# A decoder layer on one core: three pools opened and closed in nested order, TensorE's order in the output projection taken from the program, four late sums formed in the accumulation bank

## The chip, the core and the metric

The kernel runs on one core of one Trainium2 chip. A core has five engines with a queue of instructions each: TensorE (PE, matrix products; its weight loads are shown apart as PEld), VectorE (DVE), ScalarE (ACT), GpSimd (POOL) and SyncE (SP), whose queue here issues the transfers. The metric is the device time of one execution in microseconds (us), as the median of several timed runs. Beside the timed runs there is one profiled execution, whose trace gives each instruction's start and length. SBUF is the core's working memory; PSUM holds the accumulation banks, of which the kernel uses eight of 128x512 float32 (pools `psa` and `psb`, four each).

## What is computed

One layer over 1024 rows (tokens) of width 1024, in float32. Cut to its core:

```python
h = rms_norm(x, mix_norm)
z = h @ w_in                                  # eight groups of columns
o_gla = silu(gr) * rms_norm(gla_chunked(gq, gk, gv, log_a), gla_norm)   # 4 heads
o_swa = swa_sink_attention(rms_norm(sq), rms_norm(sk), sv, sinks)       # 8 heads
x = x + concat([o_gla, o_swa]) @ w_out        # the output projection
h2 = rms_norm(x, ffn_norm)
a, b = split(causal_dwconv(h2 @ w_up, conv_w, conv_b))
return x + (silu(a) * b) @ w_down
```

## The kernel before

**Tiling.** Rows are worked on in eight tiles t = 0 to 7 of 128 rows. A float32 operand is split into a high part (a cast on ACT) and a low part (value minus high part, on DVE or POOL): that is `split` (lines 102 to 107), and every product is three passes (high by high, high by low, low by high). A product of a 128x512 tile with four 128-deep pieces of weight is therefore 12 matmuls.

**Stages.** First the projections of the two mixers with the mixers woven in (the stage of `unit_r`, the gate's projection, is the last of them), then the output projection, then the second norm, then the gated MLP ("up" and "down").

**The output projection** is one level of Strassen's scheme in Winograd's form: rows t = 0..3 and 4..7 are the two halves of the rows, the halves of the inner dimension are the two mixers' outputs, and the halves of the columns are 512 wide. Instead of eight products of quarter size there are seven, P1 to P7, each for i = 0..3 (row tiles i and i + 4). Their left factors are pieces of `o` and sums of them (`o_left`, line 806), their right factors pieces and sums of `w_out`, loaded by `load_local`, `load_b22`, `load_b21`, `load_b22_late`, summed by `wo_sums` and `wo_t4` and split by `o_weight` into the places of O_PLACE (slots 0 to 9 of the weight memory, or pieces (j, i) of the three tiles `ex`). P6, P5 and P3 accumulate onto P1's bank, so that bank must have been read before P6 is written into it.

**Adds.** The residual rows x are loaded into `acc` (`load_acc`, 512 KB for each t), and after each product DVE adds the bank to one half of an `acc` row tile (line 827). `gate_tr` transposes the gated output of tile t (four transposes) and forms for t > 3 the differences and sums that are left factors; `o_sum` and `o_sum4` form and split the others.

**The second norm.** When P3 of i (or P4) has been added, row tile t = i (or i + 4) is complete. `norm2_stat` squares and sums it on ACT, `rms_scale` gives the factor by one small operation on DVE (line 176) and a power on POOL (line 178); `norm2_rows` multiplies row, factor and norm weight; `norm2_tr` transposes the result (eight transposes on PE); for t > 3 `norm2_sums` forms the sums that the up projection, again seven products, needs as right factors: nine operations on DVE, six on ACT, one on POOL. The normalized row tiles share two buffers (tag `n2h`); those of t > 3 are held until their `norm2_sums` has read them. The first products of the up projection are P1 and P2 of column chunks 0 and 1; chunk 0's P3 needs the last `norm2_sums`, that of t = 7.

**What sets the order.** Each piece of work is put down with a due time by `at(time, f, ...)`; times are in units of about 5.2 us, O is the start of the output projection, TU = O + 14 that of the up projection, and TR that of the gate's projection. The program emits pieces by due time; a planner then orders every engine's instructions by its own estimate of when they can run, so that the order on an engine can differ from that of the program unless two instructions are tied (`pin`, `behind`). On the chip every engine runs its queue in that fixed order.

**Memory.** SBUF is a stack from the left and one from the right, in pools that are opened and closed in order. The left pool `gl` holds the mixers' small tiles; when it is closed (`open_acc`, line 702, due at O - 0.05) its place goes to `ex` and to `acc` of t = 0..5. The right pools `gl_q` and `pvg` hold `qo` and `vg`, the mixers' outputs; when they are closed (`open_late`, line 710) their place goes to the last `acc` pair, the third `ex` and, in a pool `ph`, to the normalized rows. A new tile waits for the last readers of the tiles that lay in its place.

Of the kernel before, what the change touches and what calls it, by code (L numbers as in the profile page):

```python
# [17 lines left out]
P = 128  # L18
# [16 lines left out]
def hymba_layer_kernel(ctx, tc, x, mix_norm, w_in, w_alpha2, b_alpha, gla_norm,  # L35
# [19 lines left out]
    def bank(name):  # L55
# [4 lines left out]
        for which, starts in (("a", ("oP1", "oP7_3", "oP4_3", "n2pt_4", "n2pt_5_0", "n2pt_2_1", "n2pt_3")),  # L60
                              ("b", ("oP", "n2pt"))):
            if name.startswith(starts):
                return ps[which].tile([P, 512], F32, tag="b", name=name)
# [80 lines left out]
    def const_a():  # L144
        disti = gl.tile([P, 512], F32, tag="k2", name="disti", bufs=K2)[:, 0:256].bitcast(I32)
# [20 lines left out]
    rn = gl.tile([P, 2, NT], F32, name="rn")  # L166
# [42 lines left out]
    def norm2_stat(t):  # L209
        pn, acc = fin["pn"], fin["acc"][t]  # L210
        h = fin["h", t] = fin["ph"].tile([P, D], F32, tag="n2h", name=f"n2h_{t}", bufs=2)
# [4 lines left out]
    def norm2_rows(t):  # L216
        h, acc, r = fin["h", t], fin["acc"][t], fin["r", t]
        if t % 4 < 3:
            act.activation(h, acc, AF.Copy, scale=r[:, 0:1])
            for c in halves:  # L220
                pool.tensor_mul(h[:, c], h[:, c], fin["ffn"][:, c])  # L221
            return
# [4 lines left out]
    def norm2_tr(t):  # L227
        h = fin["h", t]
        if t < 4:
# [3 lines left out]
            pool.tensor_sub(tr_dst(t, 0, 1, True), b11, tr_dst(t, 0, 0, True).bitcast(F32))  # L233
# [124 lines left out]
    vv = gh.tile([P, NT, P], F32, tag="vv", name="vv", bufs=1)  # L358
# [7 lines left out]
    wa_raw = gl.tile([P, 512], F32, tag="k2", name="wa_raw", bufs=K2)[:, 0:256]  # L366
    pool.memset(wa_raw, 0.0)
    glan = gl.tile([P, 1], F32, name="glan")
# [17 lines left out]
    def k2_tile(name):  # L386
        return gl.tile([P, 512], F32, tag="k2", name=name, bufs=K2)
# [254 lines left out]
    def gla_o(t):  # L642
# [13 lines left out]
        grs[t] = rms_scale(ss, P, 4, f"g{t}", gl, "gr", 8)  # L656
# [9 lines left out]
    def gate_tr(t, gs):  # L666
# [12 lines left out]
        i = t - 4  # L679
        split(l32, big[:, t, 4:8, 0, :], big[:, t, 4:8, 1, :])  # L680
        dve.scalar_tensor_tensor(g32, pv, glan, l32, op0=ALU.mult, op1=ALU.subtract)
        dve.tensor_add(qo[:, i, :], qo[:, i, :], vg[0][:, t, :])
# [18 lines left out]

    def open_acc():
# [3 lines left out]
        fp = ctx.enter_context(tc.tile_pool(name="fp", reuse_waits="tile", bufs=1))  # L706
        fin["pair"] = [fp.tile([P, 2, D], F32, name=f"acc{i}") for i in range(3)]
        fin["acc"] = [fin["pair"][t // 2][:, t % 2, :] for t in range(6)]

    def open_late():  # L710
        st.close()
        x2 = ctx.enter_context(tc.tile_pool(name="x2", reuse_waits="tile", bufs=1))
        fin["pair"].append(x2.tile([P, 2, D], F32, name="acc3"))
        fin["acc"] += [fin["pair"][3][:, t, :] for t in range(2)]
        fin["ex"].append(x2.tile([P, 4, 4, 2, P], F32R, name="ex2"))
        fin["sn"] = ExitStack()
# [757 lines left out]
```

## Time and profile before

| what | us |
|---|---|
| median of the timed runs | 1005.75 (1005.57 to 1005.81, 3 runs) |
| the profiled execution, its own time | 1004.07 |
| its span in the trace | 1002.4 |
| PE busy in the span | 974.7 |
| PE busy in the 100 us from 300 to 400 | 85.1 |
| PE busy in the 100 us from 500 to 600 | 100.0 |

The page of the profile shows one execution: busy time by engine, the span in 40 slices (each digit a tenth), the transfers, the chain of work that ended last, and the costliest groups of instructions. A line such as "L821" is line 821 of the kernel. In the timeline and the groups a release in brackets, as in "[5.37 <-DVE acc L827]", is the time for which the engine stood idle before the piece and what ended that wait. PE's matmuls are pipelined, so their durations overlap; the distance from start to start is what one costs. "PEclk" is the clock that PE was granted, as a share of full speed.

### The profile page before, as it was taken

Reading aid. Unit: us, or ns where it says so; the run is one execution under the profiler, and the core shown is the slowest. Engines: PE = TensorE matmul, PEld = TensorE weight load, DVE = VectorE, ACT = ScalarE, POOL = GpSimd, SP = SyncE. Lnnn points to the kernel's source line nnn. Section 1 sums busy time; section 2 is a strip of 40 time slices with the busy share of each in tenths; the row PEclk is TensorE's granted clock in tenths of the full one; section 3 lists DMA queues with packets and bytes.
Section 4 is the critical chain, followed back from the end, with each engine's and each line's share of the span. In section 5 each row is a group of like instructions: output and inputs, shape, how many; then the busy total and the mean of one; then the engine's idle time right before and its main releaser. Section 6 shows DMA issues by size and latency. Waiting matters only on the chain.

```text
span 1002.4 us, 13932 instructions
## 1 busy us (share of the span) xinstructions
PE 974.7 (97%) x4915; PEld 844.4 (84%) x4915; DVE 815.6 (81%) x1350; ACT 506.7 (51%) x1035; POOL 673.4 (67%) x557
## 2 busy tenths in 40 slices
PE   8999999999997978999999999999999999999998
PEld 6888888888886866878888888888888888888887
DVE  6877767766468567698998989898989999898986
ACT  5637655445354356554454545545454545455451
POOL 5593132324687556787889788787878797888760
PEclk9999999999998988999999999999999999999999
DMA  6152123032007201211112221212121212222104
GB/s 225 64 151 73 46 55 93 22 86 64 1 1 275 62 0 43 85 35 59 41 60 60 65 63 43 84 43 84 43 69 37 64 42 65 63 64 63 43 22 168
DMA packets 67540, 68.23 MB, mean 68 GB/s; under 512 B 4650, under 2 KB 52237, under 8 KB 67470
## 3 DMA queue, kind: packets, MB, share of 16 engines
q1 hardware_dynamic: 63484, 62.35, 20.2%
q10 hardware_dynamic: 3986, 4.99, 2.1%
q8 instruction: 39, 0.64, 0.3%
q14 instruction: 31, 0.25, 0.1%
HBM read 58.41 MB, written 4.19 MB: 62 GB/s over the span
## 4 chain that ended last, share of the span: by engine, by line
PE 75%; DVE 9%; POOL 7%; issue 3%; DMA 3%; ACT 2%; ACTq 0%; SPq 0%; POOLq 0%; DVEq 0%
PE fb L969 35%; PE dn_P L1150 17%; PE dg L350 4%; PE dr L350 4%; PE dv L350 3%; PE oP L821 2%; PE pv L536 1%; PE dl L1179 1%; PE fb L1179 1%; DVE ex L107 1%; DMA qraw<-in_w_in_dram 1%; POOL n2h L221 1%; PE go L646 1%; PE ga L637 1%; POOL ex L107 1%
## 5 line engine op out<-in xcount | busy, mean ns | idle before, releaser
L1150 PE MATMUL dn_P<-dw,dg 128*128 128x512 f32 x840 | 205.1, 381 | 1.4 <-DVE acc L1154 0.7
L1154 DVE TENSOR_TENSOR acc<-acc,dn_P 128x1024 f32<-128x1024 f32 x140 | 169.3, 1210 | 30.9 <-PE dn_P L1150 30.9
L1150 PEld LDWEIGHTS dn_P<-dw,dg 128*128 128x128 f32 x840 | 157.2, 189 | 27.5 <-DVE acc L1154 3.2
L107 POOL TENSOR_TENSOR dw<-dn,dw 128x512 fp32r<-128x512 f32 x50 | 64.6, 1291 | 35.6 <-ACT dw L104 35.6
L976 DVE SCALAR_TENSOR_TENSOR ua<-fb,cc,ua 128x511 f32<-128x511 f32 (+1 forms) x84 | 61.8, 739 | 1.2 <-ACT ua L981 0.8
L969 PE MATMUL fb<-big,A11w 128*128 128x512 f32 x252 | 58.8, 381 | 1.1 <-ACT e L1025 1.1
L969 PE MATMUL fb<-big,S1w 128*128 128x512 f32 x252 | 58.6, 379 | 0.0
L969 PE MATMUL fb<-big,A12w 128*128 128x512 f32 x252 | 58.2, 379 | 0.1
L969 PE MATMUL fb<-big,S4w 128*128 128x512 f32 x252 | 58.1, 379 | 0.0
L512 POOL TENSOR_TENSOR pr<-pr,sm 128x512 f32<-128x512 f32 x16 | 17.3, 1080 | 60.7 <-DVE sm L511 33.9
L969 PE MATMUL fb<-ex,S2w 128*128 128x512 f32 x252 | 58.0, 379 | 0.0
L969 PE MATMUL fb<-ex,S3w 128*128 128x512 f32 x252 | 57.8, 379 | 0.0
L969 PE MATMUL fb<-ex,A22w 128*128 128x512 f32 x252 | 57.8, 379 | 0.0
L981 ACT ACTIVATE ua<-fb,cc 128x512 f32<-128x512 f32 x42 | 32.7, 778 | 46.2 <-DVE fb L1029 30.1
L969 PEld LDWEIGHTS fb<-big,A11w 128*128 128x128 f32 x252 | 47.7, 190 | 8.2 <-ACT e L1025 1.5
L969 PEld LDWEIGHTS fb<-big,A12w 128*128 128x128 f32 x252 | 47.5, 189 | 7.0 <-ACT b L232 0.3
L969 PEld LDWEIGHTS fb<-ex,S2w 128*128 128x128 f32 x252 | 47.6, 189 | 6.8
L969 PEld LDWEIGHTS fb<-big,S1w 128*128 128x128 f32 x252 | 47.6, 189 | 6.8
L969 PEld LDWEIGHTS fb<-ex,S3w 128*128 128x128 f32 x252 | 47.6, 189 | 6.8
L969 PEld LDWEIGHTS fb<-big,S4w 128*128 128x128 f32 x252 | 47.6, 189 | 6.8
L969 PEld LDWEIGHTS fb<-ex,A22w 128*128 128x128 f32 x252 | 47.6, 189 | 6.8
L107 POOL TENSOR_TENSOR A22w<-up,A22w 128x512 fp32r<-128x512 f32 x22 | 30.0, 1364 | 31.4 <-ACT A22w L104 31.3
(486 smaller groups left out, 2596.8 us busy)
## 6 DMA issues: line engine op xcount, KB each, us to landing
up<-in_w_up_dram SPq DMA_DIRECT2D x44, 512.0 KB, 3.9
dn<-in_w_down_dram SPq DMA_DIRECT2D x22, 512.0 KB, 3.4
acc<-in_x_dram SPq DMA_DIRECT2D x8, 512.0 KB, 6.1
out_dram<-acc SPq DMA_DIRECT2D x15, 256.0 KB, 2.7
xt<-in_x_dram SPq DMA_DIRECT2D x7, 512.0 KB, 3.4
vraw<-in_w_in_dram SPq DMA_DIRECT2D x4, 512.0 KB, 3.7
graw<-in_w_in_dram SPq DMA_DIRECT2D x4, 512.0 KB, 3.8
qt<-qt ACTq DMA_DIRECT2D x16, 128.0 KB, 2.2
```

The source lines that it names most:

```text
L107: (eng or pool).tensor_sub(lo, src, hi.bitcast(F32))
L221: pool.tensor_mul(h[:, c], h[:, c], fin["ffn"][:, c])
L350: pe.matmul(pb[:, :n], lhsT=big[:, t, k, ra, :], rhs=two_streams(ws[k][:, rb, :n]), start=(k == 0 and i == 0), stop=(k == KD - 1 and i == 2))
L512: pool.tensor_tensor(pr, pr, den[:, hs].rearrange("p (j o) -> p j o", o=1).broadcast_to((P, 4, P)), ALU.mult)
L536: pe.matmul(pbs[i][HALF[g]], lhsT=vv[rows, t - 1 + b, HALF[g]], rhs=rhs[rows, :, HALF[i]], start=start, stop=stop)
L821: pe.matmul(pb, lhsT=left[:, k, ra, :], rhs=two_streams(ow[name, k][:, rb, :]), start=(onto is None and k == 0 and n == 0), stop=(k == 3 a ...
L969: pe.matmul(pb, lhsT=w[:, ra, k, :], rhs=b_operand(bn, k, rb).rearrange("p t (h c) -> p t c h", h=2), start=(onto is None and i == 0), sto ...
L976: dve.scalar_tensor_tensor(dst, src, w, dst, op0=ALU.mult, op1=ALU.add)
L981: act.activation(u[:, a:z], y[:, a:z], AF.Identity, bias=b, scale=w2)
L1150: pe.matmul(pb[:, i], lhsT=g[:, ra, c:c + P], rhs=two_streams(w[:, rb, :]), start=(onto is None and n == 0), stop=(n == 2), skip_group_che ...
L1154: dve.tensor_add(acc, acc, pb.rearrange("p i (c h) -> p i h c", h=2))
L1179: pe.matmul(pb[:, c0:c1], lhsT=g[:, ra, (t % 4) * P:(t % 4 + 1) * P], rhs=two_streams(w[:, rb, c0:c1]), start=(ch == NCH - 2 and i == 0), ...
```

## The change

The pools: `open_acc` moves from O - 0.05 to TR + 2.0. So that `gl` can be closed then, four kinds of small tiles with late readers (`k2`, `rn`, `glan`, the factors `gr`) move into the right pool `gh`, and `vv` moves from `gh` into `gl`. In its place `xp` holds two `ex` tiles and `acc` of t = 0..3; `acc` of t = 4..7 and the third `ex` come in `x2`, opened at O + 2.2; the normalized rows are in `pn`, opened at O + 4.2. Rows 0 to 3 of x are loaded from TR + 2.05, rows 4 to 7 from O + 2.25; the adds of P7 for i = 0 and 1 are put behind that (`o_adds`). P1's weights are split at TR + 2.2 into pieces of `ex`. The loads of B21 and the late B22 are due at O + 4.3 and O + 4.4.

The late sums: for t > 3 `gate_tr` subtracts in the bank itself, splits from it the left factor of P6, and adds and subtracts the bank to `qo` and `vg`. The splits of that factor in `o_sum` and the four subtractions on POOL in `o_sum4` go.

The norm: `norm2_rows` is now two operations of DVE (row by factor by weight) for every t; before, for t % 4 < 3, it was one on ACT and two on POOL. For t = 3 one low part goes from POOL to DVE.

The order: from O to TU + 0.07 each PE instruction is tied to the one before it in the program, so that PE's order there is that of the due times. The transposes of the second norm get due times of their own, and those of the gate's last tile come between P1 of i = 1 and P1 of i = 2.

The diff, with lines of context left out:

```diff
-        for which, starts in (("a", ("oP1", "oP7_3", "oP4_3", "n2pt_4", "n2pt_5_0", "n2pt_2_1", "n2pt_3")),
+        for which, starts in (("a", ("oP1", "oP4_3", "n2pt_4", "n2pt_5_0", "n2pt_3")),
...
     def const_a():
-        disti = gl.tile([P, 512], F32, tag="k2", name="disti", bufs=K2)[:, 0:256].bitcast(I32)
+        disti = gh.tile([P, 512], F32, tag="k2", name="disti", bufs=K2)[:, 0:256].bitcast(I32)
...
-    rn = gl.tile([P, 2, NT], F32, name="rn")
+    rn = gh.tile([P, 2, NT], F32, name="rn")
...
         pn, acc = fin["pn"], fin["acc"][t]
-        h = fin["h", t] = fin["ph"].tile([P, D], F32, tag="n2h", name=f"n2h_{t}", bufs=2)
+        h = fin["h", t] = pn.tile([P, D], F32, tag="n2h", name=f"n2h_{t}", bufs=2)
...
         h, acc, r = fin["h", t], fin["acc"][t], fin["r", t]
-        if t % 4 < 3:
-            act.activation(h, acc, AF.Copy, scale=r[:, 0:1])
-            for c in halves:
-                pool.tensor_mul(h[:, c], h[:, c], fin["ffn"][:, c])
-            return
...
             act.copy(b11, trs["n2", t, 0])
-            pool.tensor_sub(tr_dst(t, 0, 1, True), b11, tr_dst(t, 0, 0, True).bitcast(F32))
+            if t < 3:
+                pool.tensor_sub(tr_dst(t, 0, 1, True), b11, tr_dst(t, 0, 0, True).bitcast(F32))
+            else:
+                tr_lo(t, 0, "n2", True)
...
     la = gh.tile([P, NT, 256], F32, tag="la", name="la", bufs=1)
-    vv = gh.tile([P, NT, P], F32, tag="vv", name="vv", bufs=1)
+    vv = gl.tile([P, NT, P], F32, name="vv")
...
     wa = gl.tile([P, 256], F32R, name="wa")
-    wa_raw = gl.tile([P, 512], F32, tag="k2", name="wa_raw", bufs=K2)[:, 0:256]
+    wa_raw = gh.tile([P, 512], F32, tag="k2", name="wa_raw", bufs=K2)[:, 0:256]
     pool.memset(wa_raw, 0.0)
-    glan = gl.tile([P, 1], F32, name="glan")
+    glan = gh.tile([P, 1], F32, name="glan")
...
     def k2_tile(name):
-        return gl.tile([P, 512], F32, tag="k2", name=name, bufs=K2)
+        return gh.tile([P, 512], F32, tag="k2", name=name, bufs=K2)
...
         dve.tensor_copy(v, pb)
-        grs[t] = rms_scale(ss, P, 4, f"g{t}", gl, "gr", 8)
+        grs[t] = rms_scale(ss, P, 4, f"g{t}", gh, "gr", 8)
...
         i = t - 4
+        dve.scalar_tensor_tensor(pv, pv, glan, l32, op0=ALU.mult, op1=ALU.subtract)
+        s2 = fin["ex"][1][:, (i + 2) % 4]
+        split(pv, s2[:, :, 0], s2[:, :, 1], dve)
         split(l32, big[:, t, 4:8, 0, :], big[:, t, 4:8, 1, :])
-        dve.scalar_tensor_tensor(g32, pv, glan, l32, op0=ALU.mult, op1=ALU.subtract)
-        dve.tensor_add(qo[:, i, :], qo[:, i, :], vg[0][:, t, :])
+        dve.tensor_add(qo[:, i, :], pb, qo[:, i, :])
+        dve.tensor_sub(vg[0][:, i, :], vg[0][:, i, :], pb)
...
+    def open_pair(pl, i):
+        fin["pair", i] = pl.tile([P, 2, D], F32, name=f"acc{i}")
+        fin["acc"][2 * i:2 * i + 2] = [fin["pair", i][:, t, :] for t in range(2)]
+
...
         fin["ex"] = [xp.tile([P, 4, 4, 2, P], F32R, name=f"ex{j}") for j in range(2)]
-        fp = ctx.enter_context(tc.tile_pool(name="fp", reuse_waits="tile", bufs=1))
-        fin["pair"] = [fp.tile([P, 2, D], F32, name=f"acc{i}") for i in range(3)]
-        fin["acc"] = [fin["pair"][t // 2][:, t % 2, :] for t in range(6)]
+        fin["acc"] = [None] * NT
+        for i in range(2):
+            open_pair(xp, i)
...
         x2 = ctx.enter_context(tc.tile_pool(name="x2", reuse_waits="tile", bufs=1))
-        fin["pair"].append(x2.tile([P, 2, D], F32, name="acc3"))
-        fin["acc"] += [fin["pair"][3][:, t, :] for t in range(2)]
+        for i in range(2, 4):
+            open_pair(x2, i)
         fin["ex"].append(x2.tile([P, 4, 4, 2, P], F32R, name="ex2"))
-        fin["sn"] = ExitStack()
-        fin["ph"] = fin["sn"].enter_context(tc.tile_pool(name="ph", reuse_waits="tile", bufs=1))
...
         w_late["pool"] = swp.enter_context(tc.tile_pool(name="wb", reuse_waits="tile", bufs=1, side="right"))
+        fin["sn"] = ExitStack()
...
     def load_b22(c2):
-        load_gated("T1", 1, c2, raw_tile("wog1") if c2 else gh.tile([P, 1024], F32, tag="vv", name="wog0", bufs=1))
+        load_gated("B22", 1, c2, raw_tile(f"wog{c2}"))
...
     def wo_sums(k2):
-        dve.tensor_sub(wo["T3", k2], wo["T1", k2], wo["T3", k2])
+        b22 = wo["B22", k2]
+        dve.tensor_sub(wo["T3", k2], b22, wo["T3", k2])
...
         dve.tensor_add(t2, wo["T3", k2], wo["B11", k2])
-        dve.tensor_sub(wo["T1", k2], wo["T1", k2], t2)
+        dve.tensor_sub(wo["B11", k2], b22, t2)
...
     def load_b21(c2):
-        load_gated("B21", 0, c2, fin["ph"].tile([P, D], F32, tag="n2h", name=f"wob21_{c2}", bufs=2))
+        load_gated("B21", 0, c2, fin["pn"].tile([P, D], F32, tag="n2h", name=f"wob21_{c2}", bufs=2))
...
-    O_PLACE = {"P1": (4, 5, 6, 7), "P7": (8, 0, 1, 2), "P6": (4, 5, 6, 7), "P5": ((2, 0), (2, 1), (1, 3), 3),
-               "P2": (4, 5, 6, 7), "P3": ((0, 2), (2, 2), (1, 2), (0, 3)), "P4": (3, 9, (2, 3), (1, 3))}
-    O_FROM = {"P1": "B11", "P6": "T2", "P5": "T1", "P7": "T3", "P4": "T2", "P2": "B21", "P3": "B22"}
+    O_PLACE = {"P1": ((0, 0), (0, 1), (0, 2), (0, 3)), "P7": (8, 0, 1, 2), "P6": (3, 4, 5, 6),
+               "P5": (7, (1, 2), (1, 3), (2, 0)), "P2": (3, 4, 5, 6), "P3": ((0, 2), (2, 2), (1, 2), (0, 3)),
+               "P4": (7, 9, (2, 3), (1, 3))}
+    O_FROM = {"P1": "B11", "P6": "T2", "P5": "B11", "P7": "T3", "P4": "T2", "P2": "B21", "P3": "B22"}
...
-    def o_sum(j, i):
-        src = (qo[:, i, :], vg[0][:, i + 4, :])[j].rearrange("p (k c) -> p k c", k=4)
-        dst = fin["ex"][j][:, (i + 2) % 4]
-        split(src, dst[:, :, 0], dst[:, :, 1], dve)
+    def o_sum1(i):
+        dst = fin["ex"][0][:, (i + 2) % 4]
+        split(qo[:, i, :].rearrange("p (k c) -> p k c", k=4), dst[:, :, 0], dst[:, :, 1], dve)
...
     def o_sum4(i):
-        pool.tensor_sub(vg[0][:, i, :], vg[0][:, i, :], vg[0][:, i + 4, :])
...
-        def add(t, half):
-            part = fin["acc"][t][:, half * 512:half * 512 + 512].rearrange("p (h c) -> p h c", h=2)
-            dve.tensor_add(part, part, halves_of(pb))
-
+        if (name, i) not in (("P7", 0), ("P7", 1)):
+            o_adds(name, i, pb)
+
+    def o_adds(name, i, pb=None):
+        if pb is None:
+            pb = psb["o", name, i]
...
                          "P7": ((4, 1), (4, 0)), "P4": ((4, 0),)}[name]:
-            add(i + dt, half)
+            part = fin["acc"][i + dt][:, half * 512:half * 512 + 512].rearrange("p (h c) -> p h c", h=2)
+            dve.tensor_add(part, part, halves_of(pb))
...
         t = 4 * th + 2 * j
-        acc = fin["pair"][t // 2][:, :, nh * 512:(nh + 1) * 512].rearrange("p i (h c) -> p i h c", h=2)
+        acc = fin["pair", t // 2][:, :, nh * 512:(nh + 1) * 512].rearrange("p i (h c) -> p i h c", h=2)
...
         at(TR + t, unit_r, t)
-        at(O + (0.005 * t - 0.045 if t < 6 else 2.4), load_acc, t)
+        if t < 4:
+            at(TR + 2.05 + 0.01 * t, load_acc, t)
+        else:
+            at(O + 2.25 + 0.005 * t, load_acc, t)
...
         at(s + 2.7, gla_o, t)
-        at(TR + t + 1.3, lambda tt=t: gate_tr(tt, psb.pop(("r", tt))))
-    at(O - 0.05, open_acc)
+        at(TR + t + 1.3 if t < 7 else O + 0.75, lambda tt=t: gate_tr(tt, psb.pop(("r", tt))))
+    at(TR + 2.0, open_acc)
     for k2 in range(2):
-        at(TR + 1.6 + 0.2 * k2, load_local, k2)
-        at(TR + 1.7 + 0.2 * k2, load_b22, k2)
-        at(TR + 2.3 + 0.2 * k2, wo_sums, k2)
-        at(O + 2.35, load_b21, k2)
-        at(O + 3.35, load_b22_late, k2)
-        at(O + 5.3, wo_t4, k2)
-    at(O + 2.3, open_late)
-    at(O + 3.3, open_norm2)
-    at(O + 3.4, load_ffn)
+        at(TR + 1.6 + 0.05 * k2, load_local, k2)
+        at(TR + 1.7 + 0.9 * k2, load_b22, k2)
+        at(TR + 2.5 + 0.7 * k2, wo_sums, k2)
+        at(O + 4.3 + 0.02 * k2, load_b21, k2)
+        at(O + 4.4, load_b22_late, k2)
+        at(O + 5.4, wo_t4, k2)
+    at(O + 2.2, open_late)
+    at(O + 4.2, open_norm2)
+    at(O + 4.5, load_ffn)
...
         eng = dve if k % 2 else pool
-        at(TO - 0.9 + 0.1 * k, o_weight, "P1", k, dve)
-        at(TO - 0.45 + 0.1 * k, o_weight, "P7", k, eng)
-        at(O + 2.02 + 0.05 * k, o_weight, "P6", k, eng)
-        at(O + (4.02 if k == 2 else 3.02 + 0.05 * k), o_weight, "P5", k, pool)
+        at(TR + 2.2 + 0.05 * k, o_weight, "P1", k, dve)
+        at(TO - 0.6 + 0.1 * k, o_weight, "P7", k, eng)
+        at(TO + 0.1 * k, o_weight, "P6", k, eng)
+        at(O + (2.3, 3.52, 4.02, 3.0)[k], o_weight, "P5", k, pool)
         at(O + 5.02 + 0.05 * k, o_weight, "P2", k, pool)
-        at(O + 6.02 + 0.05 * k, o_weight, "P3", k, eng)
+        at(O + (7.01 if k == 2 else 6.02 + 0.05 * k), o_weight, "P3", k, dve if k == 2 else eng)
...
         at(O + 0.5 * i, o_product, "P1", i)
-        at(O + 0.51 + 0.02 * i, o_sum, 1, i)
-        at(O + 1.51 + 0.02 * i, o_sum, 0, i)
-        at(O + 2.2 + 0.02 * i, o_sum4, i)
+        at(O + 2.02 + 0.02 * i, o_sum1, i)
+        at(O + 0.51 + 0.5 * i, o_sum4, i)
...
             at(O + 2 + 0.5 * i, o_product, "P7", i)
+            at(O + 2.6 + 0.05 * i, o_adds, "P7", i)
...
             at(u + 0.005, norm2_rows, t)
-            if t < 7:
-                at(u + 1.4, norm2_tr, t)
-            if 4 <= t < 7:
-                at(u + 1.51, norm2_sums, t)
+    for t, n in ((0, 19), (4, 20), (1, 22), (5, 24), (2, 26), (6, 27), (3, 28)):
+        at(O + 0.5 * n - 0.002, norm2_tr, t)
+        if t > 3:
+            at(O + 0.5 * n + 0.01, norm2_sums, t)
...
     at_us(-12, behind, first_sums)
-    at_us(0.28, norm2_tr, 7)
+    at_us(0.15, norm2_tr, 7)
...
         tu += MM
-    for _, _, f, a in sorted(ev, key=lambda e: e[:2]):
+    last_pe = None
+    for time, _, f, a in sorted(ev, key=lambda e: e[:2]):
+        n = len(nc.cur_bb.bb.instructions)
         f(*a)
+        if O <= time < TU + 0.07:
+            for ins in nc.cur_bb.bb.instructions[n:]:
+                if ins.engine == mybir.EngineType.PE:
+                    if last_pe:
+                        tc.add_manual_dep(ins, last_pe, mybir.DependencyInfo(
+                            mybir.DependencyClass.NoSync, mybir.DependencyReason.DATA), reason="order of the program")
+                    last_pe = ins.name
```

## The prediction

> **What bounds the kernel now.** I read the page first: engines, then slices, then the stretches around the slices that stand out.
>
> ```profile
> span 1002.4 us, 13932 instructions
> ...
> PE   8999999999997978999999999999999999999998
> ...
> PEclk9999999999998988999999999999999999999999
> ```
> ```profile
> 300.00:350.00 50.00, 44.63 (x203) 38.52 (x202) 36.77 (x46) 21.04 (x38) 33.11 (x24) 0.93 0.48 168
> 350.00:400.00 50.00, 40.44 (x186) 33.92 (x185) 34.43 (x56) 31.45 (x56) 32.42 (x28) 0.86 0.07 22
> ...
> 500.00:600.00 100.00, 100.00 (x463) 87.07 (x463) 91.22 (x119) 51.28 (x87) 82.48 (x62) 1.00 0.22 64
> ```
>
> PE is the bound: it is full in the MLP (100.00 of 100), and the diff leaves the matmuls alone. The stretch from 300 to 400, output projection and second norm, is the exception: 14.9 us idle, and the granted clock falls to 0.86. The waits of PE there name three causes:
>
> ```profile
> PE oP L821 <- DVE acc L827: 5.4, 1, 5.4
> PE n2pt L242 <- POOL n2h L221: 4.9, 1, 4.9
> PE n2pt L276 <- DVE n2h L224: 4.5, 2, 3.4
> ```
>
> So PE waits 5.4 us for an add of residual rows, then 9.4 us for normalized rows. PE's timeline tells what the stretch would take without them:
>
> ```profile
> 289.24 8.23 PE L821 MATMUL oP<-oP1w,big 128*128 128x512 f32 x37
> ...
> 310.83 12.49 PE L821 MATMUL oP<-oP6w,ex 128*128 128x512 f32 x48 [5.37 <-DVE acc L827]
> ...
> 333.53 2.75 PE L821 MATMUL oP<-oP2w,big 128*128 128x512 f32 x12
> 336.12 2.75 PE L821 MATMUL oP<-ex,big 128*128 128x512 f32 x12
> ...
> 358.59 1.04 PE L276 MATMUL n2pt<-ident,n2h 128*128 128x128 f32 x8
> 359.38 2.84 PE L821 MATMUL oP<-oP2w,big 128*128 128x512 f32 x12
> ...
> 396.24 1.04 PE L242 MATMUL fb<-ident,n2h 128*128 128x128 f32 x8
> ```
>
> From start to start a product costs 2.59 (333.53 to 336.12), eight transposes 0.79 (358.59 to 359.38). P6 and P5, eight products after the first wait, should take 20.72 and take 22.70 (310.83 to 333.53): 1.98 lost to the slower clock. From the first P1 to the end of the last tile's transposes 107.8 us pass (289.24 to 397.03). In them are 28 products (72.5), four transposes of the gate (0.4), 21 matmuls of the up projection (4.5) and 64 transposes (6.3): 83.7. So **24 us are lost, 14.8 idle and 9.3 to clock**. That is the most the change can win.
>
> **The change part by part.** *Earlier residual rows.* The rows of the first wait:
>
> ```profile
> SPq L811 <- DVE vg L681: 55.2, 1, 55.2
> ```
> ```profile
> 301.24 2.96 SPq L811 DMA_DIRECT2D acc<-in_x_dram  x6
> 314.36 0.89 SPq L760 DMA_DIRECT2D wob<-in_w_out_dram  x2
> ```
> ```profile
> acc<-in_x_dram SPq DMA_DIRECT2D x8, 512.0 KB, 6.1
> ```
> ```profile
> 255.79 1.06 PE L649 MATMUL go<-s_mid,qbd 128*128 128x128 f32 x8
> ```
>
> SP sat 55.2 us on the first load because `glan`, in the pool to be closed, was read last by line 681. Landing takes 6.1 us, and DVE adds P1 only then. With the late readers in another pool, the last readers of `gl` are the mixer of t = 7, whose matmuls end at 256.8: x lands some 20 us before P1 starts. What now queues behind these four loads on SP is `wog1`, which P7's weights need some 20 us later: covered. P1's four splits move to that time too, beside the gate's products. P6 follows P7 directly, at 289.24 + 6 products + 0.36 = 305.1 instead of 310.83. Rows 4 to 7 wait for `vg`, whose last reader is the last `o_sum4`: line 681 ends at 301.2 now, as the issue shows, and a cast and a split follow, so I take 303; they land by 309, and P5, their first taker, starts at 315.5. The six us between cover a DVE queue that stands at P7's deferred adds. If the cover went, P5 would stall by the excess.
>
> *Late sums.* POOL loses four subtractions, DVE gets four from the bank and loses none of its splits: 4 x 0.60 on DVE beside PE's products, nothing on the path. The gate's last transposes move behind the second P1 (294.4) and need `gs` of POOL:
>
> ```profile
> 293.84 1.73 POOL L663 TENSOR_TENSOR gs<-gs,vg 128x512 f32<-128x512 f32 x1
> ```
>
> It ends at 295.6 now, with subtractions of the removed kind ahead of it. Between no wait and 1.2 us I take none.
>
> *Later weights.* B21's load moves from `qo`'s place into `gh`'s, which is free when P5's weights have been split. Its queue on SP has x ahead of it and B22, the norm weight and the MLP's first columns behind. The second P6 ends at 310.3, and a POOL split follows, so I put the issue at 312 instead of 314.36: 2.4 earlier, where PE comes 5.7 earlier still. The chain behind it is POOL's:
>
> ```profile
> 319.54 4.79 POOL L778 TENSOR_TENSOR wot<-wob,wot 128x1024 f32<-128x1024 f32 x2
> ...
> 331.83 2.52 POOL L107 TENSOR_TENSOR ex<-wob,ex 128x512 fp32r<-128x512 f32 x2
> ...
> 335.59 1.63 POOL L107 TENSOR_TENSOR oP4w<-wot,oP4w 128x512 fp32r<-128x512 f32 x1 [1.25 <-ACT oP4w L104]
> ```
>
> P4's last POOL weight ended at 337.2. Shifted by 2.4 and with one of P3's POOL splits (1.3, half of the 2.52) given to DVE it ends at 333.5; PE wants it at 331.0 as the first piece, at 332.3 as the third. Bounds 0 and 2.5; I take **1.6** of delay for all that follows.
>
> *Rows of the norm, and DVE.* ACT loses six copies and POOL twelve multiplications; DVE gets twelve operations. With stall and slow clock gone PE needs per i three and a half products and two sets of transposes, 10.6 us. What DVE needs:
>
> ```profile
> 355.61 0.70 DVE L259 TENSOR_TENSOR n2pt<-n2pt,b 128x512 f32<-128x512 f32 x1 [1.58 <-ACT n2h L257]
> 356.22 0.68 DVE L107 TENSOR_TENSOR big<-n2pt,big 128x512 fp32r<-128x512 f32 x1
> ...
> 383.93 3.42 DVE L224 SCALAR_TENSOR_TENSOR n2h<-acc,n23r,ffn 128x512 f32<-128x512 f32 x2 [0.84 <-POOL n23r L178]
> ...
> 390.93 1.41 DVE L224 SCALAR_TENSOR_TENSOR n2h<-acc,n27r,ffn 128x512 f32<-128x512 f32 x2
> 392.25 0.69 DVE L259 TENSOR_TENSOR n2pt<-n2pt,b 128x512 f32<-128x512 f32 x1
> ...
> 398.81 0.69 DVE L259 TENSOR_TENSOR fb<-fb,b 128x512 f32<-128x512 f32 x1
> ```
> ```profile
> 386.76 2.95 POOL L221 TENSOR_TENSOR n2h<-n2h,ffn 128x512 f32<-128x512 f32 x2
> 390.08 0.55 POOL L178 TENSOR_TENSOR n27r<-n27v,mhalf 128x1 f32<-128x1 f32 x1 [0.37 <-DVE n27v L176]
> 396.87 1.27 POOL L107 TENSOR_TENSOR ex<-n2h,ex 128x512 fp32r<-128x512 f32 x1 [6.24 <-ACT ex L104]
> ```
>
> An operation from the bank costs 0.60 from start to start; a row operation 0.66 when POOL idles (two in 1.32 at 390.93) and 1.71 when POOL works beside it (383.93). [...]
>
> The mark is the first DVE operation of the last `norm2_sums`, at 398.81 now, since the MLP hangs on it:
>
> ```profile
> 403.37 1.28 POOL L107 TENSOR_TENSOR ex<-n2h,ex 128x512 fp32r<-128x512 f32 x1 [3.97 <-ACT ex L104]
> 404.72 1.28 POOL L903 TENSOR_TENSOR S<-up 128x512 f32<-128x512 f32 x1
> ```
> ```profile
> 411.03 2.75 PE L969 MATMUL fb<-ex,S2w 128*128 128x512 f32 x12
> ```
>
> POOL splits that tile's sum, at once begins chunk 1's sums, and PE's P6 of chunk 1 starts 12.2 us after the mark. Whatever PE gains before, from here it moves with the mark.
>
> When does DVE reach it? PE comes to the transposes of t = 4 after 20 products, 0.36 and 0.79, at 289.24 + 53.0 + 1.6 = 343.8, and their first sum runs 1.2 later, at 345.0. From there to the mark DVE has 27 operations of three `norm2_sums` (16.2), four low parts (2.4), nine adds (5.4), eleven row operations (7.3), five small ones (0.4) and two weight splits (1.2): **32.9**, to 377.9. Thirteen of these read SBUF twice and cost 1.05 more beside POOL: between 0 and 13.6. POOL has about a quarter of that time filled for certain (powers, lows, one split for each tile) and up to half with the MLP's first weights; at 30% it is **4.0**. The mark falls at 381.9, **16.9 earlier**. PE's path alone would bring it at about 374.8, 24 earlier.
>
> Sum: 1004.07 - 16.9 = 987.2 for the profiled execution; the median of the runs stood 1.7 above it, so 1005.75 - 16.9 = **988.9 us**.
>
> **The rivals.** *PE stays the bound.* DVE's row operations find POOL idle and use the gaps before 345; the mark is then PE's, and all 24 us are won: 981.7. For it: DVE stood idle for 15.6 of the 50 us from 350 to 400. Against: per i DVE has 11.3 us of work (nine sums 5.4, four rows 2.6, four adds 2.4, lows and small ones 0.9), 15.5 when the rows meet POOL, against PE's 10.6.
>
> *The first wait is replaced and nothing is won.* The gate's last tile waits for `gs` as long as P6 did (7.4 with the clock), and all thirteen operations meet POOL: 377.9 + 7.4 + 13.6 = 398.9, 1005.8. Against it: `gs` is 1.2 late at most by its row.
>
> *Slower: the two buffers.* Beside the rows above it needs these:
>
> ```profile
> L213 ACT ACTIVATE n2h<-acc 128x1024 f32<-128x1024 f32 x8 | 8.5, 1062 | 8.2 <-DVE acc L827 6.6 <-PE n2pt L276 1.6
> ```
> ```profile
> 368.95 0.70 DVE L259 TENSOR_TENSOR n2pt<-n2pt,b 128x512 f32<-128x512 f32 x1 [2.00 <-ACT n2h L257]
> ```
>
> The row tiles share two buffers, and a tile of t > 3 holds one until its sums are done. If the fixed order leaves tiles 4, 5, 6, 7 following each other in one buffer, each step is sums, POOL's split, square, power, rows and transposes: 5.4 + 1.3 + 1.1 + 0.6 + 3.4 + 1.8 = 13.6 when the rows meet POOL, plus what DVE does in between. The mark is 345.0 plus three steps, so it is later than 398.81 from a step of 17.9 on. At 19.3 it is 402.9: 1009.8. For it: the sums of t = 4, 5, 6 started at 355.61, 368.95 and 392.25, steps of 13.3 and 23.3. Against: the next was 6.6, so tile 7 had the other buffer.
>
> **How the numbers follow.** Forecast with its bounds (mark from 377.9 to 391.5, and up to 0.9 later with P4's upper bound): 984.9 to 999.3, chance 0.65. PE-bound: 0.15. Replaced wait: 0.10, half of it within 2 us of the old time, half a small gain. Slower: 0.10. A difference of 0.2%, 2 us, is what a measurement of this kernel can tell. So faster 0.85, same 0.05, slower 0.10. Forecast and PE-bound case together hold 0.80: the range is 982 to 999.
>
> **What would show it.** Right: the wait for `acc` is gone; PE's order is P1, P1, the gate's transposes, P1, P1, P7; DVE is over 85% busy from 345 to the mark; the remaining waits of PE are transposes that wait for L224 and the first up product after the last sums. Wrong: a long wait for P2's or P4's weights, PE waiting at the gate's transposes, or a square that waits for a row buffer. If POOL's splits of the MLP's weights all fall between 345 and 382, the time is nearer 995.

## The result, and the profile after

| | before | after |
|---|---|---|
| median of the timed runs, us | 1005.64 (1003.72 to 1005.81, 5 runs) | 1000.15 (998.75 to 1001.43, 5 runs) |
| ratio | | 0.9947, interval 0.9932 to 0.9962 |
| the profiled execution, its span | 1004.07, 1002.4 | 1001.43, 999.7 |

The change makes the kernel 5.5 us faster. The forecast was 988.9 us, with a range of 982 to 999: the sign was right, the size is a third of the 16.9 us.

The windows of the changed kernel (columns: stretch, its length, busy time of PE, PEld, DVE, ACT, POOL, granted clock, DMA share, GB/s):

```profile
300.00:350.00 50.00, 48.68 (x230) 41.49 (x229) 33.36 (x46) 19.23 (x35) 25.92 (x19) 1.00 0.34 116
350.00:400.00 50.00, 40.38 (x185) 33.68 (x184) 45.10 (x71) 26.77 (x50) 17.32 (x16) 0.90 0.08 22
500.00:600.00 100.00, 100.00 (x465) 87.22 (x464) 91.36 (x119) 50.16 (x85) 84.86 (x64) 1.00 0.20 58
```

The first half is healed: PE is busy for 48.68 of 50 us, where it was 44.63, at full clock. The second half is as it was: 40.38, where it was 40.44, while DVE rose from 34.43 to 45.10 and POOL fell from 32.42 to 17.32. PE's waits of the changed kernel (total, number, longest) say for what:

```profile
PE n2pt L240 <- DVE n2h L219: 5.7, 4, 2.5
PE fb L274 <- DVE n2h L219: 3.3, 1, 3.3
PE n2pt L274 <- DVE n2h L219: 1.2, 1, 1.2
...
PE ogt L667 <- POOL gs L661: 0.7, 1, 0.7
PE oP L825 <- DVE acc L838: 0.6, 1, 0.6
```

The wait of 5.4 us for an add has gone; 0.7 at the gate and 0.6 at an add have come. The waits of transposes for normalized rows were 4.9 and 4.5, 9.4 in all, and are 5.7, 3.3 and 1.2: 10.2. They are all on DVE now.

PE's timeline of the changed kernel:

```profile
290.76 5.43 PE L825 MATMUL oP<-ex,big 128*128 128x512 f32 x24
296.85 0.66 PE L667 MATMUL ogt<-ident,gs 128*128 128x128 f32 x4 [0.67 <-POOL gs L661]
...
307.71 10.52 PE L825 MATMUL oP<-oP6w,ex 128*128 128x512 f32 x48
...
328.43 2.75 PE L825 MATMUL oP<-oP2w,big 128*128 128x512 f32 x12
...
333.89 1.79 PE L825 MATMUL oP<-oP4w,big 128*128 128x512 f32 x6
...
343.34 1.29 PE L274 MATMUL n2pt<-ident,n2h 128*128 128x128 f32 x8 [1.18 <-DVE n2h L219]
...
347.05 1.28 PE L240 MATMUL n2pt<-ident,n2h 128*128 128x128 f32 x8
...
384.89 1.94 PE L274 MATMUL fb<-ident,n2h 128*128 128x128 f32 x8 [3.33 <-DVE n2h L219]
386.65 4.94 PE L976 MATMUL gb<-big,A11w 128*128 128x512 f32 x12
391.43 2.75 PE L976 MATMUL gb<-big,A12w 128*128 128x512 f32 x12
394.02 1.04 PE L240 MATMUL fb<-ident,n2h 128*128 128x128 f32 x8
...
407.85 2.75 PE L976 MATMUL fb<-ex,S2w 128*128 128x512 f32 x12
```

P6 comes without a wait. The transposes of t = 4 are at 347.05. From those of t = 3 at 384.89 on, PE no longer stands: they, not the last sums, are where the end is set.

One measure serves for all kernels below: **the stretch** from PE's first P1 to its P6 of chunk 1, 290.76 to 407.85 here. It is counted from P1 because P1's own start scatters: it was 290.76 in this profile and 289.23 in a second one of the same kernel. In the stretch lie 28 products and seven up products at 2.59 (90.7), 64 transposes (6.3) and the gate's four (0.4): 97.3 of work at full clock. What goes beyond is lost: in PE's waits, to a lower granted clock, and in small gaps that the list of waits leaves out. That is 24.5 us before (121.8 less 97.3), of which 14.8 are waits; 19.8 after (117.1 less 97.3), of which 11.5 are waits.

DVE's timeline of the changed kernel shows why PE waits:

```profile
332.04 1.10 DVE L107 TENSOR_TENSOR A11w<-up,A11w 128x512 fp32r<-128x512 f32 x1 [1.82 <-ACT A11w L104]
...
334.76 0.68 DVE L107 TENSOR_TENSOR A12w<-up,A12w 128x512 fp32r<-128x512 f32 x1
...
338.29 0.69 DVE L910 TENSOR_TENSOR s<-up 128x512 f32<-128x512 f32 x1 [2.25 <-DMA up<-in_w_up_dram]
...
339.69 0.68 DVE L838 TENSOR_TENSOR acc<-acc,oP 128x512 f32<-128x512 f32 x1
...
342.44 1.42 DVE L219 SCALAR_TENSOR_TENSOR n2h<-acc,n20r,ffn 128x512 f32<-128x512 f32 x2
...
344.59 2.44 DVE L219 SCALAR_TENSOR_TENSOR n2h<-acc,n24r,ffn 128x512 f32<-128x512 f32 x2
...
348.92 0.15 DVE L176 TENSOR_SCALAR n21v<-n2ss 128x1 f32<-128x1 f32 x1 [1.30 <-ACT n2h L213]
...
350.01 1.40 DVE L219 SCALAR_TENSOR_TENSOR n2h<-acc,n21r,ffn 128x512 f32<-128x512 f32 x2
...
352.52 0.69 DVE L257 TENSOR_TENSOR n2pt<-n2pt,b 128x512 f32<-128x512 f32 x1
...
373.15 3.36 DVE L219 SCALAR_TENSOR_TENSOR n2h<-acc,n26r,ffn 128x512 f32<-128x512 f32 x2
...
384.00 1.41 DVE L219 SCALAR_TENSOR_TENSOR n2h<-acc,n23r,ffn 128x512 f32<-128x512 f32 x2
```

The product that completes row tile 0 ends at 333.9 on PE. Its add waits until 339.69, because DVE's queue stands at work for the MLP: at the split of A11 (`up_operand`) for 1.82 us, then at `first_sums` for 2.25 us, until a load of `w_up` has landed. SP issues that load late:

```profile
334.31 0.99 SPq L898 DMA_DIRECT2D up<-in_w_up_dram  x2
```

PE takes nothing of that work before 386.65; the first to read one of the sums is ACT's cast of S4, at 370.67. Behind it the row's square, power, row operations and transposes all come late; PE waits 1.18 at 343.34. The first sums, those of t = 4, begin at 352.52, where the forecast had 345.0. That is 5.5 us behind their transposes: until then DVE is at adds, at a wait of 1.30 for the square of t = 1, and at the rows of t = 1.

### The profile page after: what moved, and what is told of

It reads as the page before. It is cut to its first block, busy times and chain, and to the rows that moved or that the text cites. A ratio compares the mean times of both kernels' runs of the same rounds, so it can differ in the third digit from the quotient of the medians.

```text
span 999.7 us, 13937 instructions
## 1 busy us (share of the span) xinstructions
PE 974.2 (97%) x4915; PEld 842.5 (84%) x4915; DVE 825.3 (83%) x1368; ACT 500.0 (50%) x1029; POOL 647.5 (65%) x539
## 4 chain that ended last, share of the span: by engine, by line
PE 77%; DVE 9%; POOL 5%; issue 3%; DMA 2%; ACT 2%; ACTq 0%; SPq 0%; POOLq 0%; DVEq 0%
PE fb L976 35%; PE dn_P L1157 17%; PE dg L348 4%; PE dr L348 4%; PE dv L348 3%; PE oP L825 3%; PE pv L534 1%; DVE n2h L219 1%; PE dl L1186 1%; PE fb L1186 1%; PE dq L848 1%; DMA up<-in_w_up_dram 1%; PE go L644 1%; PE ga L635 1%; DMA wob<-in_w_out_dram 1%
## 5 line engine op out<-in xcount | busy, mean ns | idle before, releaser
L107 POOL TENSOR_TENSOR dw<-dn,dw 128x512 fp32r<-128x512 f32 x50 | 64.6, 1292 | 35.6 <-ACT dw L104 35.6
L510 POOL TENSOR_TENSOR pr<-pr,sm 128x512 f32<-128x512 f32 x16 | 17.3, 1080 | 61.4 <-DVE sm L509 36.0
```

The lines of the kernel that those rows point to most:

```text
L107: (eng or pool).tensor_sub(lo, src, hi.bitcast(F32))
L510: pool.tensor_tensor(pr, pr, den[:, hs].rearrange("p (j o) -> p j o", o=1).broadcast_to((P, 4, P)), ALU.mult)
```

## The experiments

Three theories stood after the result. **A**: the rows given to DVE fill it, and back on ACT and POOL they would cost less; its rival is that the way of one row (square, factor, rows, transposes) counts, which the change shortens. **B**: the loss is the place of the transposes of t = 7, behind two up products. **C**: the loss is the blocked head of DVE's queue near 335. The ratios are to the kernel before, timed beside each. The stretch comes from each profile; "lost" is the stretch less 97.3, "waits" the sum of PE's waits in it. In the stretch of "PE's order not tied" lie 14 more matmuls of the up projection, 3.0 us, which are taken off too.

| kernel | median us | ratio, interval | stretch | lost | waits |
|---|---|---|---|---|---|
| before | 1005.64 | | 121.8 | 24.5 | 14.8 |
| after | 1000.15 | 0.9947 [0.9932, 0.9962] | 117.1 | 19.8 | 11.5 |
| after, once more | 1000.74 | 0.9935 [0.9913, 0.9956] | 117.6 | 20.3 | 12.1 |
| residual rows late again | 1007.83 | 1.0026 [1.0013, 1.0039] | 123.3 | 26.0 | 15.9 |
| rows on ACT and POOL again | 1002.00 | 0.9961 [0.9944, 0.9978] | 119.2 | 21.9 | 13.7 |
| PE's order not tied | 999.22 | 0.9950 [0.9936, 0.9964] | 117.6 | 17.3 | 11.1 |
| transposes of t = 7 earlier | 998.04 | 0.9936 [0.9911, 0.9961] | 115.5 | 18.2 | 12.5 |
| rows plain | 994.81 | 0.9894 [0.9867, 0.9921] | 112.7 | 15.4 | 10.3 |
| MLP work tied behind the rows | 993.99 | 0.9895 [0.9872, 0.9918] | 111.5 | 14.2 | 8.4 |
| tied, and rows plain | 991.51 | 0.9872 [0.9856, 0.9888] | 109.2 | 11.9 | 6.9 |
| tied, sums on POOL | 997.81 | 0.9929 [0.9914, 0.9944] | 115.0 | 17.7 | 9.4 |
| tied, and t = 7 earlier | 996.29 | 0.9890 [0.9868, 0.9911] | 113.0 | 15.7 | 9.7 |
| before, tied | 1007.28 | 1.0001 [0.9982, 1.0020] | 122.7 | 25.4 | 15.2 |

### The residual rows late again

```diff
-        if (name, i) not in (("P7", 0), ("P7", 1)):
+        if name != "P1" and (name, i) not in (("P7", 0), ("P7", 1)):
...
-            at(TR + 2.05 + 0.01 * t, load_acc, t)
+            at(O + 2.28 + 0.005 * t, load_acc_tied, t)
...
+        at(O + 2.4 + 0.01 * i, o_adds, "P1", i)
```

> The changed kernel with the first part undone: rows 0 to 3 of x are loaded among rows 4 to 7, behind the last readers of vg, and P1's adds come after that. P6 then waits 4 to 7 us for P1's add again. If the chain behind is rigid, all of it arrives: 5 to 8 us slower than the changed kernel, which is what the first part is worth. If DVE's first complete row tile waits for the MLP's weights anyway (theory C), the delay is partly covered: only 1 to 3 us slower.

Measured: 1.0026. PE's timeline of this kernel has the old wait back:

```profile
311.02 4.60 PE L825 MATMUL oP<-oP6w,ex 128*128 128x512 f32 x10 [4.68 <-DVE acc L838]
```

The 4.68 us there come through undiminished: by the ratios this kernel is 7.9 us slower than after, its stretch is 6.2 longer than after, and 1.5 longer than before. So the first part carries the whole gain. The rest of the change gives a little away, as far as this kernel stands for it: its rows 0 to 3 also queue behind rows 4 to 7, which is not how the kernel before loads them.

### The rows on ACT and POOL again

```diff
+        if t % 4 < 3:
+            act.activation(h, acc, AF.Copy, scale=r[:, 0:1])
+            for c in halves:
+                pool.tensor_mul(h[:, c], h[:, c], fin["ffn"][:, c])
+            return
```

> The changed kernel with norm2_rows as before (t % 4 < 3: one ACT copy, two POOL multiplications). Theory A: DVE loses twelve operations, 13.0 us in the changed kernel's trace, and the time falls by 3 to 6 us. Rival (the length of each tile's own chain bounds: copy and two multiplications take 3.7 us, two DVE operations 1.4 to 3.4): the time rises by 1 to 4 us, towards that of before.

Measured: 0.9961, a stretch 2.1 longer than after. PE's waits of this kernel:

```profile
PE n2pt L245 <- POOL n2h L221: 7.8, 2, 7.3
PE n2pt L279 <- POOL n2h L221: 3.5, 2, 2.9
```

DVE is relieved (35.3 us busy of the 50 from 350 to 400, where it was 45.1), and PE waits longer, for POOL. Theory A falls: nothing was won. Its rival agrees, but the rise is small: 1.4 us by the ratios, inside their intervals, and 2.1 by the stretch of one profile.

### PE's order not tied

```diff
-        if O <= time < TU + 0.07:
+        if False:
```

> The changed kernel without the ties of PE's order, so that the planner's order holds there. If the fixed order costs time at its end (theory B), 1 to 3 us faster; if it is what keeps PE's queue free of early blocked products, 1 to 4 us slower; if it does nothing by itself, within 1 us.

Measured: 0.9950, with nearly the interval of the changed kernel. The stretch is 0.5 longer, but holds 3.0 us more of the up projection, so the two cannot be set side by side. The ties alone do nothing to the time that these runs can tell.

### The transposes of t = 7 earlier

```diff
-    at_us(0.15, norm2_tr, 7)
+    at_us(0.05, norm2_tr, 7)
```

> The changed kernel with one due time altered: the transposes of the last row tile (t = 7) stand between the first two products of the up projection instead of behind both. Theory B (the fixed order holds the last tile back: DVE had its rows ready at 390.8 and the transposes ran at 394.0): the first DVE operation of the last norm2_sums comes about 2.6 us earlier, and the time falls by 2 to 3 us against the changed kernel. Theory A (DVE's amount of work alone sets that point): no more than 0.5 us.

Measured: 0.9936. PE's timeline of this kernel:

```profile
383.18 1.69 PE L274 MATMUL fb<-ident,n2h 128*128 128x128 f32 x8 [4.08 <-DVE n2h L219]
384.52 4.09 PE L976 MATMUL gb<-big,A11w 128*128 128x512 f32 x12
```

From P1 the mark comes 4.3 us earlier than after (100.25 for 104.56), P6 of chunk 1 only 1.6 (115.53 for 117.09). PE is full from the transposes of t = 3 on, in this kernel as after, so a mark that comes earlier finds no idle PE. Nor is the 1.6 the mark's: PE's waits are 1.0 longer here, and the slow clock took 3.0 less (see the last section). Against the changed kernel once more, 0.9935, the time is the same. Theory B holds for the mark, not for the time.

### Rows plain

One ACT copy scaled by the factor takes the place of the two DVE operations; the norm weight is left out.

```diff
-        for c in halves:
-            dve.scalar_tensor_tensor(h[:, c], acc[:, c], r[:, 0:1], fin["ffn"][:, c],
-                                     op0=ALU.mult, op1=ALU.mult)
+        act.activation(h, acc, AF.Copy, scale=r[:, 0:1])
```

> The changed kernel with norm2_rows as one ACT copy scaled by the row's factor for every t; the multiplication by the norm weight is left out. That takes sixteen operations, 15.8 us in the changed kernel's trace, from DVE. Theory A (DVE is full from 341 to 391, so its work is what the norm stage costs): the first operation of the last norm2_sums comes 8 us earlier or more, time 6 to 9 us below the changed kernel. Theory C (the adds at the head of DVE's queue are late because they stand behind splits and sums that wait for the MLP's weights): those stay late, so only 2 to 4 us are won.

Measured: 0.9894, 5.3 us below after, between the two ranges; the mark comes 4.4 earlier (100.20 from P1), where theory A wanted 8. With 16 operations fewer DVE is busy for 35.6 of the 50 us from 350 to 400, and yet PE still waits for rows:

```profile
PE fb L272 <- ACT n2h L218: 3.9, 1, 3.9
PE n2pt L238 <- ACT n2h L218: 3.8, 2, 2.8
```

DVE's load is thus a part of the cause and not the whole. The blocked head is untouched here: the first complete row is added at 338.24, 49.4 behind P1, where after has 48.9.

### The MLP's first work tied behind the rows of t = 4

The DVE operations of the splits of A11 and A12 and of `first_sums` are tied, without a wait, behind the row operations of t = 4.

```diff
+    def rows_tied(f, *a):
+        n = len(nc.cur_bb.bb.instructions)
+        f(*a)
+        for ins in nc.cur_bb.bb.instructions[n:]:
+            if ins.engine == mybir.EngineType.DVE:
+                tc.add_manual_dep(ins, rows_end["name"], mybir.DependencyInfo(
+                    mybir.DependencyClass.NoSync, mybir.DependencyReason.DATA), reason="order of the program")
...
-    at_us(-12, behind, first_sums)
+    at_us(-12, rows_tied, first_sums)
```

> The changed kernel with the two DVE splits and the four DVE sums of the MLP's first weights tied behind the row operations of t = 4 on DVE. Theory C: the add of the first complete row tile no longer waits for the load of the MLP's weights and comes at 334 to 335 instead of 339.7, the first norm2_sums starts 3 to 5 us earlier; the six operations (3.6 us) fall in DVE's full stretch, so the time falls by 1 to 3 us. Theory A: no change, since DVE has the same work.

Measured: 0.9895, where after has 0.9947: about 5 us (4 against the changed kernel once more), above the 1 to 3 expected. With the whole computation no kernel is clearly faster. PE's transposes of t = 4, and below them DVE's timeline, of this kernel:

```profile
345.35 1.04 PE L240 MATMUL n2pt<-ident,n2h 128*128 128x128 f32 x8
```
```profile
334.53 1.27 DVE L838 TENSOR_TENSOR acc<-acc,oP 128x512 f32<-128x512 f32 x2
337.02 0.15 DVE L176 TENSOR_SCALAR n20v<-n2ss 128x1 f32<-128x1 f32 x1 [1.21 <-ACT n2h L213]
...
340.10 1.41 DVE L219 SCALAR_TENSOR_TENSOR n2h<-acc,n24r,ffn 128x512 f32<-128x512 f32 x2
341.43 0.68 DVE L107 TENSOR_TENSOR A11w<-up,A11w 128x512 fp32r<-128x512 f32 x1
...
349.80 0.69 DVE L257 TENSOR_TENSOR n2pt<-n2pt,b 128x512 f32<-128x512 f32 x1
```

The first complete row is added between 334.5 and 335.8 instead of at 339.69, and the tied work finds its data there: the 1.82 and 2.25 us of standing are gone. From P1 the first sums come 2.8 us earlier (58.9 for 61.8), just under the 3 to 5 expected, the transposes of t = 3 at the end 3.9 earlier (90.3 for 94.1) and without their wait of 3.33; the slow clock that followed that wait shrinks too (the first up product takes 3.57 us from start to start for 4.78), and P6 of chunk 1 is 5.6 earlier, 3.1 of it in waits. Theory C holds: the head of the queue cost time, as forecast in kind and more in size.

### The same tie in the kernel before

The same operations, tied behind line 176 of t = 4, as the row operations of that tile ran on ACT and POOL.

> The kernel before with the same tie as the run 'tied behind rows of t=4': the four DVE instructions of the first two MLP weights' splits and of first_sums stand behind the power's input of t=4 (n24v). If DVE's blocked head is a fault that was there before the change (idle 1.96 and 1.67 us in the kernel before, the add of the first complete row at 341.38), and the norm's chain set its end too, then the complete row's add comes 3 to 5 us earlier and the time is 999 to 1002, ratio 0.995 to 0.998. If PE and ACT's squares and copies set the kernel before there, and only the change made DVE's order matter, it is 1003.5 to 1005.5, ratio 0.999 to 1.001.

Measured: 1.0001. DVE's timeline of the untouched kernel before shows the same standing at the head of the queue:

```profile
333.78 1.11 DVE L107 TENSOR_TENSOR A11w<-up,A11w 128x512 fp32r<-128x512 f32 x1 [1.96 <-ACT A11w L104]
...
340.05 0.69 DVE L903 TENSOR_TENSOR s<-up 128x512 f32<-128x512 f32 x1 [1.67 <-DMA up<-in_w_up_dram]
...
341.38 0.68 DVE L827 TENSOR_TENSOR acc<-acc,oP 128x512 f32<-128x512 f32 x1
```

With the tie the add of the complete row comes at 339.08 instead of 341.38, and waits for nothing but its product:

```profile
339.08 0.69 DVE L827 TENSOR_TENSOR acc<-acc,oP 128x512 f32<-128x512 f32 x1 [1.90 <-PE oP L821]
```

But PE's waits stay (15.2 us, before 14.8), and for the same causes. The fault stood in DVE's queue before the change and cost nothing there beyond the 2 us that these runs can tell. Between the two kernels PE came to P2 6.6 us earlier from P1 (37.7 for 44.3), and the rows came to DVE; which of the two made the fault cost, or whether it took both, wasn't tried.

### Tied, with the sums on POOL

```diff
-        sums(s1, ra[:, 0:4], rb[:, 0:4], rb[:, 4:8], dve)
-        dve.tensor_sub(ra[:, 4:8], ra[:, 4:8], ra[:, 0:4])
+        sums(s1, ra[:, 0:4], rb[:, 0:4], rb[:, 4:8])
+        pool.tensor_sub(ra[:, 4:8], ra[:, 4:8], ra[:, 0:4])
```

> e4 with the four sums of the MLP's first weights on POOL, behind the power of t = 4, where POOL stood idle. [...]

Measured: 0.9929, 3.4 us worse by ratio than the tie alone (the intervals just touch), with a stretch 3.5 longer. The forecast was 1 to 2.5 us less if DVE's work still counts, and up to 1 more if the row operations of t = 1 get longer beside POOL. DVE's timeline, and below it POOL's, of this kernel:

```profile
339.21 3.35 DVE L219 SCALAR_TENSOR_TENSOR n2h<-acc,n24r,ffn 128x512 f32<-128x512 f32 x2
...
348.06 1.42 DVE L219 SCALAR_TENSOR_TENSOR n2h<-acc,n21r,ffn 128x512 f32<-128x512 f32 x2 [1.08 <-POOL n21r L178]
```
```profile
339.04 1.28 POOL L910 TENSOR_TENSOR s<-up 128x512 f32<-128x512 f32 x1
...
347.48 0.55 POOL L178 TENSOR_TENSOR n21r<-n21v,mhalf 128x1 f32<-128x1 f32 x1
```

Beside POOL's sums the two row operations of t = 4 take 3.35 us instead of 1.41 (those of t = 1 take 1.42), and the power of t = 1 stands behind the sums and a low part of the norm. POOL was not free help.

### Tied, with the rows plain; tied, with t = 7 earlier

The two edits above with the tie; in the first of them the norm weight is left out.

> e4 (MLP's first weights tied behind t = 4) together with e2 (rows by one ACT copy, norm weight left out). If DVE's work is the next bound once its head is free, another 3 to 6 us below e4; if the two row buffers or PE's order are, within 2 us of e4.

> Tie behind rows of t=4 and the transposes of t=7 ahead of the first two up products, together. If the two losses add, 992 to 993 (ratio 0.9875 to 0.989), 1 to 1.6 us below the tie alone. If, once DVE is free early, the rows of t=7 come so late that PE waits for them in front of the up products, it is 994 to 996, no better than the tie alone or worse.

Measured: 0.9872 and 0.9890. Plain rows give 2.3 us beyond the tie by the ratios, whose intervals overlap, and by the stretch; without it they gave 5.3. So, argued from these two numbers, part of what they won there made up for the blocked head. The earlier transposes give nothing: the rows of t = 7 are not ready, and PE waits 1.05 us at them in front of the second up product. In the tied kernel with plain rows PE's longest wait is still 4.8, and ACT's timeline shows at what:

```profile
371.49 0.65 ACT L104 CAST S2w<-up 128x512 fp32r<-128x512 f32 x1
372.01 1.17 ACT L218 ACTIVATE n2h<-acc,n26r 128x1024 f32<-128x1024 f32 x1
```

The factor n26r is there at 369.6 (POOL's power starts at 369.05 and takes 0.54); the copy that uses it stands until 372.01, behind a square and a cast of the norm and two casts for the MLP's later weights (1.0 us). ACT is busy here and not blocked, but again work that is wanted later stands in front.

### The changed kernel once more

> The changed kernel once more, beside the others on one chip: 0.9935 to 0.9960 of the kernel before. It is here so that the tied kernels can be set against it on one chip; all theories say the same.

Measured: 0.9935, an interval that overlaps the first.

## Why the prediction was wrong

- **Earlier residual rows: right.** From P1 to P6 the forecast was 15.9 us, before it was 21.59; measured 16.95. Of the 1.05 missing 0.67 is the gate's wait, from its own bounds of 0 to 1.2 (forecast at 0). Undoing this step costs 6.2 us of the stretch.
- **Late sums: nothing on the path** that the trace shows, but for that wait. They were not undone by themselves.
- **Later weights: over-costed.** Forecast 1.6 of delay. P2 starts eight products to the hundredth after P6 (20.72), and P3 and P4 lose 0.3 between them (P4 starts at 333.89, two products after P2 would be 333.61).
- **DVE's way to the mark: the step that failed is its start.** "PE comes to the transposes of t = 4 ..., and their first sum runs 1.2 later, at 345.0" took PE as all that DVE waits for. Measured 352.52. Of the 7.5 us, 1.5 are P1's own scatter. From P1 the transposes came after 56.3 us instead of 54.6, and the sum 5.5 behind them instead of 1.2, since DVE's queue has the rows of t = 1, a wait of 1.30 for their square, and adds in front of it. Part of that is the head of the queue, 4.1 us of standing (1.82 and 2.25): with the tie the transposes come after 54.5 and the sum after 58.9, so the head costs 2.8 of the remaining 6.0. The other 3.2 are there with the tie too, where the sum still runs 4.5 behind its transposes; no run put the sums of t = 4 ahead of the rows of t = 1, so what that order costs stays open. The same standing is in the trace before (1.96 and 1.67); the prediction read DVE's busy time there as a sum of work and not its order.
- **DVE's work from there: nearly right.** 36.9 forecast (32.9 and 4.0 for meeting POOL), 38.9 measured, from 352.52 to 391.44. In it two pairs of row operations ran beside POOL (359.24 and 373.15) and took 2.98 and 3.36 where the other three, with POOL idle, take 1.40 to 1.41, and one sum (line 264, at 385.33 beside a POOL split) took 1.76 instead of 0.69, 4.6 us more in all; a third pair, 2.44, lies ahead of it. The 4.0 took 1.05 more for any of thirteen operations beside POOL, the author's estimate from the pairs at 383.93 and 390.93 of before. No run shows it for all thirteen: after, the two pairs cost 1.57 and 1.95 more, and the two weight splits (368.30 and 369.50) found POOL idle and took 0.68 and 0.69.
- **The mark as the only anchor: wrong.** It fell at 395.32 for 381.9: 7.5 us are the start, 2.0 the work, and 3.9 the transposes of t = 7 behind two up products. But the time does not follow the mark: after, PE is full from 384.89 on, and a mark 4.3 us earlier left the time as it was. PE waits at the transposes of every tile, and the last such wait sets the end.
- **The rivals.** PE's bound did not come: of the 19.8 us still lost 11.5 are waits and 4.7 the slow clock. The replaced wait is nearest in kind: the second half's waits did not fall (9.4 before, 10.8 after, with the one for an add), so the change won its first wait, with the slow clock behind it (1.98 us at P6 and P5), and nothing else. Two row buffers did not make it slower.

What stays open: the tied kernel wins back about 5 of the 11.3 us between forecast and result. It still loses 14.2 us, 8.4 of it in waits, 4.9 of them at the transposes of t = 6. A third buffer for rows was not tried.

## What to carry to other kernels

An engine with idle time can still be late: read what stands at the head of its queue, and whether that work is wanted soon. When a change brings another engine forward, look on the trace before for every place where the queue that it will wait for stands at a transfer or at a cast; a wait that cost nothing so far can be where the gain goes. Measure such a stretch from its own start to where PE is full again, since a mark in between can move without the end.

## What the runs showed of the hardware that was not expected

A wait of PE can cost more than itself, and how much more does not follow from its length. The windows of the changed kernel, right behind the wait of 3.33 us at 384.89:

```profile
386.00:391.00 5.00, 5.00 (x14) 3.95 (x14) 4.65 (x8) 3.19 (x6) 1.09 (x2) 0.51 0.00 1
391.00:396.00 5.00, 5.00 (x29) 4.44 (x28) 1.82 (x4) 1.66 (x3) 0.00 (x0) 1.00 0.01 2
```

PE is full in both, but the granted clock is 0.51 in the first and 1.00 in the second: the first up product took 4.78 us from start to start (386.65 to 391.43) instead of 2.59. In windows of 0.25 us this slow spell lasts 6.8 us, to 391, with a granted clock down to 0.50. An earlier one after, to 380.75, lasts 3.4; the three of the profile before last 6.8 each. Behind the longer wait of 4.08, in the kernel with the transposes of t = 7 earlier, the same product took 4.10 (384.52 to 388.62). A wait of 1.70 was followed by slow matmuls too (358.43, tied with the sums on POOL: the next product took 4.07), one of 2.79 was not (371.52, rows plain: the eight transposes took 0.85). Where the tie took the wait of 3.33 away the product took 3.57 (382.42 to 385.99), of which 0.64 is a wait of its own.

PE's busy time times what the granted clock lacked gives the price of the slow clock in the stretch: 7.6 us before and 4.7 after. From the timelines, the time from start to start beyond that at full clock, less waits, is 5.1 us for the slow matmuls after and 3.1 tied, but 2.1 with the transposes of t = 7 earlier, whose waits are longer than those after (12.5 for 11.5). So these runs give no fixed price for a wait. What sets where a slow spell starts and how long it lasts they do not show.
